# Compression's first product in float32 from unsplit weights, and three moves of work around it

## The chip, the cores and the metric

One NeuronCore of a Trainium2 chip runs the whole program. The metric is device time in microseconds; the median of the timed runs counts, and lower is better.

## What is computed

The program is two transformer layers with attention of several kinds, then two more with other kinds and feed-forward parts, on 256 tokens of width 1024, all in float32. The change lies in the first mixer, native sparse attention (NSA), and in what is loaded around it. Cut to that:

```python
def adaln_norm(x, c, g, w_ada, b_ada):
    mod = jax.nn.silu(c) @ w_ada + b_ada
    shift, scale, gate = jnp.split(mod, 3, axis=-1)
    h = rms_norm(x, g) * (1.0 + scale[:, None, :]) + shift[:, None, :]
    return h, gate[:, None, :]

def nsa_mixer(h, w_in, pe_k, pe_v, ck_w1, ck_w2, cv_w1, cv_w2, w_out):
    u = h @ w_in                       # q, k_c, v_c, k_s, v_s, k_w, v_w, z, gate logits
    ...
    n_cmp = (T - CMP_LEN) // CMP_STRIDE + 1                       # 15 blocks of 32 tokens
    cmp_idx = CMP_STRIDE * np.arange(n_cmp)[:, None] + np.arange(CMP_LEN)[None, :]

    def compress(a, pe, w1, w2):       # w1: 2048 x 256, w2: 256 x 64
        blk = a[:, cmp_idx] + pe[:, None, :]
        blk = jnp.moveaxis(blk, 3, 2).reshape(B, n_cmp, G, CMP_LEN * DH)
        return jax.nn.silu(blk @ w1) @ w2

    k_cmp = compress(k_c, pe_k, ck_w1, ck_w2)
    v_cmp = compress(v_c, pe_v, cv_w1, cv_w2)
    ...
```

`blk @ w1` is a product of 30 rows (15 blocks, two key heads) by 2048 by 256, once for keys (m = 0) and once for values (m = 1).

## The kernel before, in words

**Split weights.** Large products run in fp32r, a faster reading of float32, on pairs: a weight unit of 128 x 1024 floats (512 KB) is loaded into a raw tile (`wraw`, 5 buffers), ScalarE copies it to a high part (`whi`), VectorE subtracts to get a low part (`wlo`), 8 buffers each. Three matmuls (high by high, low by high, high by low) make one product. `specs` lists all units in the order of use; `make` loads and splits the next one, and `pump` runs ahead as long as fewer than 8 units are made and not yet used. All loads go through SyncE's queue (SP), which issues in order and waits at a load whose buffer is not yet free.

**The order of work.** The program is written with priorities (`first(n)`), and a scheduler then fixes the order on each engine before the program runs. Each engine takes its instructions strictly in that order. A move of one line can therefore move others.

**The stages that matter here.** First stage: for each of 8 slices k of the width, the modulation weights `ada_w` (two raw tiles) and the first columns of `w_nsa` (keys, values, gates, half of the queries) are loaded, `modulate(k)` makes a slice of the normed input on ScalarE and VectorE, `multiply(k)` adds its products to six PSUM banks `accp`. Then `dense_cols` makes the other half of the queries ("the q product"), with `kvd` copies and transposes, `blk` (keys and values in blocks, plus positions), and `k_side` and `q_side` (rotation on VectorE, the rotated queries' sum on GpSimd, transposes on TensorE into PSUM banks 6 and 7 in turn, copies out by ScalarE or VectorE). Then come `compress(0)`, `compress(1)` and between them the first "z product" (`zs`). After `compress(1)` the pools are closed, and `ada_rows` loads 24 pieces of 512 KB (`ar`), each multiplied on VectorE (L660) beside the attention.

In `compress` of the kernel before, each of 16 slices j gives three matmuls with the blocks (128 x 30) as the loaded weights and 256 columns of `w1` streaming; the result, 30 x 256, goes through silu and two transposes to `hT`.

In the rows, `wh`/`wl` are the high and low parts of a unit, `wr` its raw tile, `kvd` the doubled keys and values, `q` the queries (their first half, `qf`, plain, their second, `qq`, rotated), `kd` rotated keys, `rt` parts of a rotation, `th`/`h` silu, `m`/`mask` the attention masks, `ar`/`ac` modulation rows.

## Time and profile before

| | |
|---|---|
| time, median of 3 runs | 1000.05 us (994.53 to 1003.32) |
| the profiled execution | 994.04 us, span of its trace 992.3 us |
| TensorE busy (PE) | 934.9 us, 94% of the span |
| VectorE (DVE), ScalarE (ACT) | 701.5 us (71%), 538.8 us (54%) |
| DMA | 177.66 MB, mean 179 GB/s |

Busy time is the time in which an engine has an instruction in work; matmuls overlap, so a busy TensorE isn't at its peak. The granted clock is TensorE's: 1.00 is full speed (2.4 GHz), 0.50 half of it.

### The profile page before, as it was taken

What the parts mean: (1) busy time and instruction counts of PE and PEld (TensorE: products, weight loads), DVE (VectorE), ACT (ScalarE), POOL (GpSimd) and SP (SyncE); (2) the same over time, 40 slices, a digit from 0 to 9 for tenths busy, and PEclk for the clock granted to TensorE, in tenths of its full rate; (3) what the DMA queues carried; (4) which work ended last, traced back from release to release, by engine and by line L of the source; (5) the groups of instructions that cost most, each with busy time, mean ns of one, the idle gap of its engine ahead of it and who ended that gap; (6) DMA issues with size and microseconds to landing.
All of it is one profiled execution on the core that took longest, in us unless ns stands there. A gap on an engine that the chain in (4) does not pass through costs nothing.

```text
span 992.3 us, 14766 instructions
## 1 busy us (share of the span) xinstructions
PE 934.9 (94%) x5316; PEld 783.7 (79%) x5316; DVE 701.5 (71%) x1454; ACT 538.8 (54%) x1062; POOL 40.6 (4%) x49
## 2 busy tenths in 40 slices
PE   5997998899999998999799999999999899999996
PEld 4876786687778877967788888887997688888885
DVE  5888899858777768586857565677466676665655
ACT  5584567834545626486346554435676355555540
POOL 1003000001120001000000000000000000000000
PEclk9998798999999999999999999999999999999999
DMA  9996787334855425632356554655635243565541
GB/s 288 304 311 217 221 269 253 108 106 151 261 202 182 149 66 197 236 111 86 95 203 212 170 184 159 241 181 151 221 132 152 90 167 126 193 235 170 182 137 43
DMA packets 106169, 177.66 MB, mean 179 GB/s; under 512 B 8816, under 2 KB 40688, under 8 KB 106096
## 3 DMA queue, kind: packets, MB, share of 16 engines
q1 hardware_dynamic: 106096, 176.72, 54.6%
q8 instruction: 42, 0.69, 0.3%
q14 instruction: 31, 0.25, 0.1%
HBM read 175.65 MB, written 1.05 MB: 178 GB/s over the span
## 4 chain that ended last, share of the span: by engine, by line
PE 77%; DVE 11%; ACT 5%; DMA 4%; issue 2%; SPq 1%; POOL 0%; DVEq 0%; ACTq 0%; POOLq 0%
PE ps L279 15%; PE ps L239 13%; PE ps L240 13%; PE ps L243 13%; PE ps L280 8%; DVE wl L211 2%; DMA wr<-in_ada_w_dram 2%; PE ps L469 2%; PE ps L320 1%; DVE ac L660 1%; PE ps L839 1%; PE ps L525 1%; ACT e L482 1%; PE ps L297 1%; PE ps L298 1%
## 5 line engine op out<-in xcount | busy, mean ns | idle before, releaser
L211 DVE TENSOR_TENSOR wl<-wr,wh 128x1024 fp32r<-128x1024 f32 (+5 forms) x276 | 319.6, 1195 | 78.7 <-ACT wh L210 77.3
L210 ACT ACTIVATE wh<-wr 128x1024 fp32r<-128x1024 f32 (+5 forms) x276 | 270.6, 1021 | 72.4 <-PE ps L243 21.2
L279 PE MATMUL ps<-xhl,wh 128*128 128x512 f32 x640 | 226.5, 398 | 0.0
L239 PE MATMUL ps<-wh,xhl 128*128 128x512 f32 (+5 forms) x544 | 197.4, 375 | 4.5 <-ACT xhl L312 2.4
L240 PE MATMUL ps<-wl,xhl 128*128 128x512 f32 (+5 forms) x544 | 199.0, 368 | 0.0
L280 PE MATMUL ps<-xhl,wl 128*128 128x256 f32 x640 | 179.2, 281 | 0.0
L243 PE MATMUL ps<-wh,xhl 128*128 128x512 f32 (+5 forms) x544 | 172.9, 370 | 0.9 <-DVE xhl L313 0.6
L279 PEld LDWEIGHTS ps<-xhl,wh 128*128 128x128 f32 x640 | 120.0, 188 | 28.9
L280 PEld LDWEIGHTS ps<-xhl,wl 128*128 128x128 f32 x640 | 120.9, 189 | 1.1
L239 PEld LDWEIGHTS ps<-wh,xhl 128*128 128x128 f32 x544 | 103.6, 192 | 22.8 <-ACT xhl L312 5.1
L240 PEld LDWEIGHTS ps<-wl,xhl 128*128 128x128 f32 x544 | 104.5, 192 | 14.0 <-issue 0.2
L243 PEld LDWEIGHTS ps<-wh,xhl 128*128 128x128 f32 x544 | 99.8, 190 | 18.2 <-DVE xhl L313 2.4
L1124 ACT ACTIVATE hs<-ps 128x256 f32<-128x256 f32 x80 | 30.0, 377 | 100.1 <-PE ps L280 100.1
L1125 DVE TENSOR_TENSOR hs<-ps,hs 128x256 f32<-128x256 f32 x80 | 32.6, 420 | 68.4 <-ACT hs L1124 68.4
L243 PE MATMUL ps<-wh,hl 128*128 128x512 f32 x176 | 68.3, 390 | 0.0
L240 PE MATMUL ps<-wl,hh 128*128 128x512 f32 x176 | 68.3, 390 | 0.0
L239 PE MATMUL ps<-wh,hh 128*128 128x512 f32 x176 | 66.7, 390 | 0.0
L482 ACT ACTIVATE e<-e,sm 128x128 f32<-128x128 f32 x112 | 49.6, 445 | 12.7 <-DVE sm L476 12.6
L312 ACT ACTIVATE xhl<-ps 128x512 fp32r<-128x512 f32 x28 | 16.5, 597 | 67.9 <-PE ps L309 67.8
L476 DVE CUSTOM_DVE_ANT_0 e<-ps,mask 128x128 f32<-128x128 f32 (+1 forms) x144 | 44.1, 350 | 8.8 <-PE ps L489 4.3
L660 DVE SCALAR_TENSOR_TENSOR ac<-ar,cs,ac 128x512 f32<-128x512 f32 x56 | 42.7, 764 | 4.0 <-DMA ar<-in_ada_w_dram 3.7
L334 POOL TENSOR_TENSOR sm<-sm,nhalf 128x1 f32<-128x1 f32 x18 | 13.2, 734 | 721.3 <-DVE sm L333 721.3
(315 smaller groups left out, 1299.3 us busy)
## 6 DMA issues: line engine op xcount, KB each, us to landing
wr<-in_ffn_w_gate_dram SPq DMA_DIRECT2D x44, 512.0 KB, 4.7
wr<-in_ffn_w_up_dram SPq DMA_DIRECT2D x44, 512.0 KB, 4.7
wr<-in_ffn_w_down_dram SPq DMA_DIRECT2D x44, 512.0 KB, 5.0
ar<-in_ada_w_dram SPq DMA_DIRECT2D x32, 512.0 KB, 4.5
wr<-in_dil_w_in_dram SPq DMA_DIRECT2D x32, 512.0 KB, 4.6
wr<-in_cd_w_in_dram SPq DMA_DIRECT2D x22, 512.0 KB, 4.4
wr<-in_ada_w_dram SPq DMA_DIRECT2D x32, 256.0 KB, 4.9
...
```

The source lines that it names most:

```text
L210: act.activation(hi, raw[:, :nk * n], AF.Copy)
L211: dve.tensor_sub(lo, raw[:, :nk * n], hi.bitcast(F32))
L239: pe.matmul(p, lhsT=xt[0][:, k, :], rhs=w[0][:, kw, c], start=start and t == 0, stop=False)
L240: pe.matmul(p, lhsT=xt[0][:, k, :], rhs=w[1][:, kw, c], start=False, stop=False)
L243: pe.matmul(p, lhsT=xt[1][:, k, :], rhs=w[0][:, kw, c], start=False, stop=stop and t == n - 1)
L279: pe.matmul(p, lhsT=w[0], rhs=xhl[:, k].rearrange("p a t -> p (a t)"), start=k == 0, stop=False)
L280: pe.matmul(p[:, :256], lhsT=w[1], rhs=xh[:, k, :], start=False, stop=k == 7)
L476: state["dve"] = dve.tensor_tensor_reduce(out=e[:, c0:c1], in0=s[:, c0:c1], in1=added[:, 256 - (c1 - c0):], scale=-scale, scalar=3e38, op0 ...
L482: act.activation(e[:, c0:c1], e[:, c0:c1], AF.Exp, bias=n2[:, i:i + 1], scale=-1.0, accum_out=den[:, i:i + 1])
L660: dve.scalar_tensor_tensor(ac, raw[:, j, :], cs[:, k:k + 1], ac, op0=ALU.mult, op1=ALU.add)
L1124: act.activation(t[:, c], p[:, 256:], AF.Copy)
L1125: dve.tensor_add(t[:, c], p[:, :256], t[:, c])
```

## The change

Five edits. (1) The units of `ck_w1` and `cv_w1` become "whole" units: 2048 x 256 in two units a matrix, loaded as float32 straight into the buffers of `whi` and `wlo` (half of a unit in each), with no raw tile and no split; `compress` takes 2 units in place of 4. (2) The product is turned round: 128 x 128 pieces of `w1` are the loaded weights, the 30 blocks stream, in float32, 2 halves by 16 slices; silu's result is `hT` itself, so the two transposes, their copy and the split of `blk` go; factors of 0.5 move into later copies. (3) `ident`, `ccol`, `gcol` and `bcol` are issued from ScalarE's queue. (4) `w2k`, `w2v` and the masks are issued behind the last load that has been made by then; `peT` stays ahead, behind `cc`. (5) The keys and values are rotated and copied out ahead of the queries.

```diff
     ident = cp.tile([128, 128], F32, name="ident")
-    nc.sync.dma_start(ident, A["k_ident"])
+    nc.scalar.dma_start(ident, A["k_ident"])
...
-    nc.sync.dma_start(ccol, A["c_col"])
+    nc.scalar.dma_start(ccol, A["c_col"])
...
     def make():
-        W, k0, nk, cols = specs[len(made)]
+        W, k0, nk, cols, whole = specs[len(made)]
         n = sum(b - a for a, b in cols)
+        if whole:
+            parts = []
+            for i, tag in enumerate(("whi", "wlo")):
+                t = wp.tile([128, UNIT], F32R, tag=tag, bufs=NB, name=nm("ww")).bitcast(F32).rearrange("p (k n) -> p k n", n=n)
+                h = t.shape[1]
+                a, b = cols[0]
+                state["dma"] = nc.sync.dma_start(t, W[(k0 + i * h) * 128:(k0 + (i + 1) * h) * 128, a:b].rearrange("(k p) n -> p k n", p=128))
+                parts.append(t)
+            made.append(parts)
+            return
...
-    spec_cols(A["nsa_ck_w1"][0], 16, [[(0, 256)]])
-    spec_cols(A["nsa_cv_w1"][0], 16, [[(0, 256)]])
+    for name in ("nsa_ck_w1", "nsa_cv_w1"):
+        for k0 in (0, 8):
+            spec(A[name][0], k0, 8, [(0, 256)], True)
...
         nc.sync.dma_start(cc, A["k_cc"])
+        nc.sync.dma_start(peT, A["pe_T"])
     pump()
-    load_masks()
-    nc.sync.dma_start(peT, A["pe_T"])
-    for j in range(2):
-        nc.sync.dma_start(w2k[:, :, j * 64:(j + 1) * 64], A["nsa_ck_w2"][0].rearrange("(k p) n -> p k n", p=128))
-    nc.sync.dma_start(w2v, A["nsa_cv_w2"][0].rearrange("(k p) n -> p k n", p=128))
+    with behind(state["dma"]):
+        for j in range(2):
+            nc.sync.dma_start(w2k[:, :, j * 64:(j + 1) * 64], A["nsa_ck_w2"][0].rearrange("(k p) n -> p k n", p=128))
+        nc.sync.dma_start(w2v, A["nsa_cv_w2"][0].rearrange("(k p) n -> p k n", p=128))
+        load_masks()
...
-    blk = [(pB.tile([128, 16, 30], F32R, name=f"blkh{m}"), pB.tile([128, 16, 30], F32R, name=f"blkl{m}")) for m in range(2)]
+    blk = [pB.tile([128, 16, 30], F32, name=f"blk{m}") for m in range(2)]
...
-            act.activation(hi, f, AF.Copy)
-            dve.tensor_sub(lo, f, hi.bitcast(F32))
...
     with first(SINK):
         for tok in range(2):
-            q_side(tok, 1, accp[4 + tok])
-        for tok in range(2):
-            k_side(accp[tok], tok, 256, 384, 0)
             p = accp[2 + tok]
             act.activation(vS[:, tok, :], p[:, 0:128], AF.Copy)
             k_side(p, tok, 128, 256, 1)
             act.activation(vW[:, tok, :], p[:, 256:384], AF.Copy)
             act.activation(gates[:, tok, :], p[:, 384:432], AF.Tanh, scale=0.5)
+        for tok in range(2):
+            q_side(tok, 1, accp[4 + tok])
+        for tok in range(2):
+            k_side(accp[tok], tok, 256, 384, 0)
...
     def compress(m, tp):
-        ws = get(4)
+
+        ws = get(2)
         p = ps("c")
-        for j in range(16):
-            w, l = ws[j // 4], blk[m]
-            for i, (a, b) in enumerate(((0, 0), (0, 1), (1, 0))):
-                pe.matmul(p[:30, :256], lhsT=l[a][:, j, :], rhs=w[b][:, j % 4, :],
-                          start=j == 0 and i == 0, stop=j == 15 and i == 2)
-        done(4)
-        h2 = tp.tile([128, 256], F32, tag="h2", bufs=1, name=nm("h2"))
-        silu2(p[:30, :256], h2[:30], tp)
+        for half in range(2):
+            for j in range(16):
+                w = ws[j // 8][j % 8 // 4][:, j % 4, half * 128:(half + 1) * 128]
+                pe.matmul(p[:, half * 30:(half + 1) * 30], lhsT=w, rhs=blk[m][:, j, :], start=j == 0, stop=j == 15)
+        done(2)
         hT = tp.tile([128, 2, 30], F32, tag="hT", bufs=2, name=nm("hT"))
-        p = ps("pt")
-        for j in range(2):
-            pe.transpose(p[:, j * 30:(j + 1) * 30], h2[:30, j * 128:(j + 1) * 128], ident[:30, :30])
-        act.activation(hT, p[:, :60].rearrange("p (j n) -> p j n", j=2), AF.Copy, scale=0.5)
+        silu2(p[:, :60], hT.rearrange("p j n -> p (j n)"), tp)
         return hT
```

**What the scheduler makes of it** at three places. Line numbers above 160 differ between the two kernels: L205 is now L216 and L209 (the whole units), L210 is L221, L320 is L331, L323 is L334, L812 is L821, L839 is L850, L868 is L873.

*Place 1, SP's queue* after the loads of the q product. Before:

```order
L205 DMA wr133_663<-in_nsa_ck_w1_dram 128x4x256
L205 DMA wr136_669<-in_nsa_ck_w1_dram 128x4x256
L205 DMA wr173_843<-in_nsa_ck_w1_dram 128x4x256
L205 DMA wr176_849<-in_nsa_ck_w1_dram 128x4x256
L205 DMA wr186_907<-in_nsa_cv_w1_dram 128x4x256
L205 DMA wr189_919<-in_nsa_cv_w1_dram 128x4x256
L205 DMA wr192_931<-in_nsa_cv_w1_dram 128x4x256
L205 DMA wr195_943<-in_nsa_cv_w1_dram 128x4x256
L205 DMA wr204_1018<-in_nsa_w_in_dram 128x2x512
L153 DMA ab288_1344<-in_ada_b_dram 128x1024
L205 DMA wr207_1024<-in_nsa_w_in_dram 128x2x512
```

and now:

```order
L209 DMA ww135_668<-in_nsa_ck_w1_dram 128x4x256
L209 DMA ww169_831<-in_nsa_cv_w1_dram 128x4x256
L209 DMA ww171_835<-in_nsa_cv_w1_dram 128x4x256
L209 DMA ww134_666<-in_nsa_ck_w1_dram 128x4x256
L209 DMA ww136_670<-in_nsa_ck_w1_dram 128x4x256
L780 DMA w2k_103<-in_nsa_ck_w2_dram 128x2x64 x2
L781 DMA w2v_104<-in_nsa_cv_w2_dram 128x2x64
L162 DMA m137_675<-in_k_mask_dram 128x544
L162 DMA m138_678<-in_k_mask_dram 128x544
L209 DMA ww170_833<-in_nsa_cv_w1_dram 128x4x256
L209 DMA ww172_837<-in_nsa_cv_w1_dram 128x4x256
L216 DMA wr189_927<-in_nsa_w_in_dram 128x2x512
```

Three of the four z units of the first z product now stand ahead of this piece (behind the q units), the masks and `w2` stand in it, and the fourth z unit, `wr189`, is last.

*Place 2, ScalarE* when `multiply(7)` ends. Before:

```order
L210 ACTIVATE wh122_641<-wr121_639 128x1024
L210 ACTIVATE wh125_647<-wr124_645 128x1024
L782 ACTIVATE kvd141_720<-ps11_162 128x512
L823 ACTIVATE vS_99<-ps13_164 128x128
L812 ACTIVATE q147_752<-ps15_166 128x512
L782 ACTIVATE kvd143_729<-ps12_163 128x512
L210 ACTIVATE wh128_653<-wr127_651 128x1024
L823 ACTIVATE vS_99<-ps14_165 128x128
L812 ACTIVATE q152_772<-ps16_167 128x512
L210 ACTIVATE wh131_659<-wr130_657 128x1024
```

and now:

```order
L221 ACTIVATE wh122_642<-wr121_640 128x1024
L221 ACTIVATE wh125_648<-wr124_646 128x1024
L221 ACTIVATE wh128_654<-wr127_652 128x1024
L795 ACTIVATE kvd139_714<-ps11_162 128x512
L829 ACTIVATE vS_99<-ps13_164 128x128
L795 ACTIVATE kvd141_723<-ps12_163 128x512
L221 ACTIVATE wh131_660<-wr130_658 128x1024
L829 ACTIVATE vS_99<-ps14_165 128x128
L802 ACTIVATE kvT_712<-ps140_716 64x4x127
L802 ACTIVATE kvT_712<-ps142_725 64x4x128
```

The third split (`wh128`) now stands ahead of both `kvd` copies. On TensorE the transposes of both copies now stand ahead of the whole q product; before, one stood ahead of it and one among its products.

*Place 3, ScalarE and TensorE* during the q product's end and `compress(0)`. ScalarE before, from the value weights' splits on:

```order
L210 ACTIVATE wh190_921<-wr189_919 128x1024
L210 ACTIVATE wh193_933<-wr192_931 128x1024
L812 ACTIVATE q198_949<-ps185_900 128x512
L323 ACTIVATE qp11_113<-ps155_780 128x512
L210 ACTIVATE wh196_945<-wr195_943 128x1024
L825 ACTIVATE vW_100<-ps13_164 128x128
L826 ACTIVATE gates_101<-ps13_164 128x48
L210 ACTIVATE wh205_1020<-wr204_1018 128x1024
L825 ACTIVATE vW_100<-ps14_165 128x128
L826 ACTIVATE gates_101<-ps14_165 128x48
L323 ACTIVATE kT_98<-ps160_799 128x2x128
```

and now:

```order
L334 ACTIVATE qp01_111<-ps154_776 128x512
L221 ACTIVATE wh187_917<-wr186_915 128x1024
L821 ACTIVATE q192_933<-ps179_884 128x512
L221 ACTIVATE wh190_929<-wr189_927 128x1024
L334 ACTIVATE qp11_113<-ps159_796 128x512
L334 ACTIVATE kT_98<-ps164_815 128x2x128
L221 ACTIVATE wh199_988<-wr198_986 128x1024
L334 ACTIVATE kT_98<-ps168_826 128x2x128
L221 ACTIVATE wh202_994<-wr201_992 128x1024
L334 ACTIVATE qp00_110<-ps177_872 128x512
L579 ACTIVATE th205_999<-ps197_953 128x60
```

TensorE before:

```order
L320 MATMUL ps155_780<-ident_67,q152_772 128x128 x4
L320 MATMUL ps151_766<-ident_67,q147_752 128x128 x4
L839 MATMUL ps203_969<-wh134_665,blkh0_711 30x256
L839 MATMUL ps203_969<-wl135_666,blkh0_711 30x256
L839 MATMUL ps203_969<-wh134_665,blkl0_712 30x256
L839 MATMUL ps203_969<-wh134_665,blkh0_711 30x256
L839 MATMUL ps203_969<-wl135_666,blkh0_711 30x256
L839 MATMUL ps203_969<-wh134_665,blkl0_712 30x256
```

and now:

```order
L850 MATMUL ps197_953<-blk0_707,ww133_664 128x30 x4
L850 MATMUL ps197_953<-blk0_707,ww134_666 128x30 x2
L331 MATMUL ps159_796<-ident_67,q156_788 128x128 x4
L850 MATMUL ps197_953<-blk0_707,ww134_666 128x30
L331 MATMUL ps160_802<-ident_67,q156_788 128x128 x4
L850 MATMUL ps197_953<-blk0_707,ww134_666 128x30
L850 MATMUL ps197_953<-blk0_707,ww135_668 128x30 x4
L850 MATMUL ps197_953<-blk0_707,ww136_670 128x30 x4
L850 MATMUL ps197_953<-blk0_707,ww133_664 128x30 x2
L331 MATMUL ps164_815<-ident_67,kd161_808 128x128 x2
L850 MATMUL ps197_953<-blk0_707,ww133_664 128x30 x2
L850 MATMUL ps197_953<-blk0_707,ww134_666 128x30 x4
```

On ScalarE the split `wh190` of the fourth z unit now stands ahead of the copy `qp11`, which empties the PSUM bank that TensorE's `ps164` takes next. On TensorE the transposes of the first rotated queries (before `ps151`, from `q147`) stood right ahead of the first compression product; now they stand earlier, among the q product, and those of the second token block (`q156`) and of `kd161` stand inside the compression.

## Rows read from the trace of the kernel before

**Rows 1.** Windows: busy us of PE, PEld, DVE, ACT, POOL; clock, DMA share, GB/s.
```profile
3.00:25.00 22.00, 13.34 (x50) 11.90 (x51) 13.31 (x36) 13.08 (x25) 3.36 (x6) 1.00 1.07 317
25.00:53.00 28.00, 25.15 (x139) 21.90 (x138) 24.16 (x61) 16.81 (x35) 0.00 (x0) 1.00 1.04 313
53.00:82.00 29.00, 22.86 (x113) 19.13 (x113) 25.39 (x41) 21.75 (x33) 1.70 (x2) 0.94 0.95 313
```

**Rows 2.** Chain that ended last, 30 to 125 us: start, length, what.
```profile
76.84 0.67 DVE rt L440
...
80.83 4.05 PE ps L839 x19
...
86.79 0.44 PE ps L320 x4
...
97.34 1.27 PE ps L839 x11
```

**Rows 3.** Timeline of TensorE, 50 to 112 us: start, length, instruction, [idle before].
```profile
60.29 0.65 PE L785 MATMUL ps<-ident,kvd 128*128 128x128 f32 x4
...
79.71 1.11 PE L320 MATMUL ps<-ident,q 128*128 128x128 f32 x4 [6.14 <-POOL q L447]
```

**Rows 4.** The same timeline at the end of the compression.
```profile
104.75 0.41 PE L880 MATMUL ps<-kbd,qp 128*128 128x30 f32 x2 [1.25 <-ACT kbd L860]
...
106.92 1.86 PE L868 MATMUL ps<-w2v,rep 128*120 128x64 f32 x8 [0.65 <-ACT rep L867]
109.21 1.65 PE L469 MATMUL ps<-kT,qr 64*128 64x128 f32 x8 [0.43 <-DVE cs L886]
```

**Rows 5.** Waits of SP's queue, 0 to 130 us: waiting line, releaser, us, times.
```profile
SPq L638 <- PE ps L868: 3.0, 1, 3.0
```

**Rows 6.** Windows of the attention stage, columns as in rows 1.
```profile
114.00:150.00 36.00, 36.00 (x219) 27.46 (x219) 34.47 (x113) 25.50 (x74) 0.00 (x0) 0.97 0.78 254
150.00:193.00 43.00, 38.04 (x261) 28.98 (x262) 40.06 (x153) 35.53 (x120) 0.00 (x0) 0.92 0.62 199
```

**Rows 7.** DMA issues of 0 to 210 us: count, KB each, us to landing.
```profile
m<-in_k_mask_dram SPq DMA_DIRECT2D x2, 272.0 KB, 5.2
...
w2k<-in_nsa_ck_w_dram SPq DMA_DIRECT2D x2, 64.0 KB, 4.3
...
w2v<-in_nsa_cv_w_dram SPq DMA_DIRECT2D x1, 64.0 KB, 4.6
```

**Rows 8.** Timeline of SP, its first issue and the masks.
```profile
0.73 0.39 SPq L128 DMA_DIRECT2D ident<-in_k_ident_dram  x1
...
11.08 0.91 SPq L162 DMA_DIRECT2D m<-in_k_mask_dram  x2
```

**Rows 9.** Groups by form, 50 to 125 us: count, busy us, mean ns.
```profile
L211 DVE TENSOR_TENSOR wl<-wr,wh 128x1024 fp32r<-128x1024 f32 x24 | 29.3, 1235 | 9.0 <-ACT wh L210 9.0
L210 ACT ACTIVATE wh<-wr 128x1024 fp32r<-128x1024 f32 x24 | 25.4, 1059 | 9.6 <-issue 4.0 <-PE ps L839 2.3 <-DMA wr<-in_nsa_w_in_dram 2.0
...
L796 DVE TENSOR_TENSOR blk<-kvT,peT 128x240 f32<-128x240 f32 x4 | 2.0, 563 | 0.0
```

**Rows 10.** Timeline of TensorE at full clock, 132 to 139 us.
```profile
135.81 0.39 PE L880 MATMUL ps<-kbd,qp 128*128 128x30 f32 x2
136.04 0.18 PE L881 MATMUL ps<-cmask,identb 128*128 128x30 bf16 x1
```

**Rows 11.** Timeline of ScalarE, 55 to 115 us.
```profile
56.36 1.06 ACT L210 ACTIVATE wh<-wr 128x1024 fp32r<-128x1024 f32 x1 [0.75 <-DMA wr<-in_nsa_w_in_dram]
58.68 1.06 ACT L210 ACTIVATE wh<-wr 128x1024 fp32r<-128x1024 f32 x1 [1.26 <-DMA wr<-in_nsa_w_in_dram]
```

**Rows 12.** Windows of one microsecond, and one stretch of attention, columns as in rows 1.
```profile
80.00:81.00 1.00, 1.00 (x6) 0.91 (x6) 1.00 (x2) 0.00 (x0) 0.00 (x0) 0.50 1.03 383
...
112.00:113.00 1.00, 1.00 (x7) 1.00 (x8) 0.08 (x1) 0.00 (x0) 0.00 (x0) 0.50 1.03 393
...
186.00:199.00 13.00, 11.07 (x87) 8.58 (x86) 9.75 (x39) 11.44 (x39) 0.00 (x0) 1.00 0.18 70
```

More of the change, by code (lines that the diff above doesn't have):

```diff
@@ L184, in behind, with spec @@
         return nullcontext() if ins is None else tc.issue_after(ins.ins)
-    def spec(W, k0, nk, cols):
-        specs.append((W, k0, nk, cols))
+    def spec(W, k0, nk, cols, whole=False):
+        specs.append((W, k0, nk, cols, whole))
     def spec_cols(W, nk, groups):
```

12 lines of the change are left out of this document (5 added, 7 removed).

## The prediction

> **What bounds the kernel now.** I read the windows of the first 82 us first. From 3 us on the DMA engines are full (share 0.95 to 1.07, 313 to 317 GB/s), while VectorE and TensorE are not [rows 1]: the first stage runs at the pace of its loads. Next, the chain of waits: at 76.84 it lies on VectorE (rotation of queries, behind eight splits of compression weights), and from 80.83 on TensorE [rows 2]. Between them TensorE's timeline shows the price: 6.14 us idle until 79.71, for the rotated queries' sum on GpSimd [rows 3], and after it half clock (its window of 80 to 81) [rows 12]. At the end of the compression it idles again, 1.25 and 0.65 us [rows 4]. Then SP's waits: the first `ar` load waits for L868, the last product that reads the compression's pools [rows 5], and from 114 to 193 us VectorE is busy 74.5 of 79 us [rows 6], much of it with the `ar` pieces. So the end of L868, 108.8 us [rows 4], is where a shift of this stage reaches the rest: what is won there moves all that follows. In the order of the changed kernel everything behind the first mixer stands as before, but for a handful of rows. I sum up to that point.
>
> **First stage, loads.** The masks and `w2` are issued at 11 us and later among the first stage's loads [rows 8]; they leave it: 2 x 272 + 2 x 64 + 64 = 736 KB [rows 7], at 313 GB/s 2.4 us. Bounds: 0 (if VectorE bound this stage) and 2.4; I take 2.4, as the share of 1.04 says. They come back behind the compression's key weights, beside the work of that stage. SP's issue of `ident` (0.39 us) no longer stands ahead of `x` [rows 8]: 0.4. The other three small issues, 1.2 us more at that length, I count at nothing: from 3 us on the engines are full [rows 1], so an earlier issue only lengthens the line. The Trainium skill has a rule for this (DMA: Bandwidth & Descriptors, "Issuing engines are not separate DMA queues"): loads of every issuing engine run on the same 16 engines and interleave, and a second issuer saves issue time alone. The trace agrees in that the share doesn't rise above full; if the second queue brought bandwidth, the whole 1.6 us would count. **Sum: -2.8.**
>
> **Removed waits.** Eight splits go, 1.24 us each on VectorE and 1.06 on ScalarE [rows 9], 9.9 and 8.5 us, with the two splits of `blk`. They stand ahead of the rotation that TensorE waits for; with them go the 6.1 us [rows 3]. What is late next there is below. After the idle time 19 products take 4.05 us at half clock, where eleven take 1.27 at full clock [rows 2]: 0.213 against 0.115, 1.8 us; the four transposes take 1.11 [rows 3], later 0.44 [rows 2]: 0.6 with rounding. **-8.5.** The gaps of 1.25 and 0.65 us and half clock on L868 (1.86 us for eight, half of it 0.9) go if TensorE gets there fed [rows 4]: **-2.8.**
>
> **The product turned round.** Before: 96 matmuls of 0.115 us at full clock [rows 2], 11.0. After: 64 float32 products with 128 x 128 loaded weights and 30 columns. The trace has this very form: L880, two rows each, 135.81 to 136.04 [rows 10], 0.23 us. 64 x 0.23 = 14.7. The four short transposes go, four tenths of a microsecond at the pace of rows 2. All of it is on TensorE's path: **+3.2** with rounding. A price below 0.23 has no row; the same form at half clock would be 0.46 (first rival).
>
> **New waits.** The order shows four. (a) Place 2: both `kvd` transposes wait for ScalarE, where the third q split stands first. Its weights: the two units before it landed at 56.36 and 58.68 [rows 11]; 512 KB at 313 GB/s take 1.7, so 60.4, less 2.8 is 57.6. Split 1.06 [rows 11] and a copy of half its width, about 0.6, give 59.3, the second copy and transposes 60.3. `multiply(7)` ends at 60.29 - 2.8 = 57.5 [rows 3], and eight transposes are 0.9: **+1.9** (0 if ScalarE's split were early; 3 at most). (b) The transposes of `kd` stand inside the q product's first token block. VectorE must first have `blk` (four of 0.56, 2.0 us in all [rows 9]) and rotate keys, for the second `kd` also a query block (0.67 for the first of three steps [rows 2]); TensorE comes there after 19 products of 0.23, at 64.7, the two `kd` by my count at 65.7 and 67.4: **+1.8** (0 to 3). (c) Place 3: `ps164` waits for `qp11`, which waits behind `wh190` for the fourth z unit. By the shapes in the code, what stands in SP's queue up to that unit is 24.6 MB; by rows 1 the engines move 24.8 MB between 3 and 82 us (79 us at 313 to 317 GB/s), some before 3, and start 0.4 earlier, so it lands near 80.5. Split 1.06 and copy 0.6: 82.2. TensorE comes there at 60.3 + 48 products (11.0) + 1.8 + 20 transposes (2.2, rows 2) + 18 products (4.1) = 79.4: **+2.8** (0 to 6). (d) After `compress(1)` VectorE splits one more unit (1.24) before `hT`, with ScalarE's tanh and copies after it; six z products (1.4) cover part: **+1.0.**
>
> Edits at nothing: (3)'s loads on ScalarE, which waits for `x` anyway; silu on 128 x 60 instead of 30 x 256; the moved factors; GpSimd's mask copies, now between the second and third sum of queries, with the masks there by about 77 us and the third sum not needed before 83. The whole units' loads wait for buffers that `multiply(6)` and `multiply(7)` leave at 57.5; behind them in SP's queue stands the fourth z unit of (c), nothing else that is early enough to matter.
>
> **After L868** TensorE is at half clock still: L469's eight take 1.65 us [rows 4], at full clock half of it, 0.8, and the four L880 pairs behind them, 0.25 with L881 at full clock [rows 10] and twice that here, another 1.0. If TensorE comes there fed, 1.8 go; it comes there behind gaps of 1 to 3 us, so I take half, **-0.9**.
>
> **Sum:** -2.8 - 8.5 - 2.8 + 3.2 + 1.9 + 1.8 + 2.8 + 1.0 - 0.9 = **-4.3**; with (a) to (c) at their lower bounds -10.8, at their upper ones +1.2. I keep the middle. The profiled execution, 994.04 (span 992.3 and 1.7 around it), would be near 990; it lies 6 us under the median, so against the median of 1000.05 the forecast is **996**.
>
> **Rivals.** *The float32 product runs at half clock.* 64 loads of full weights with 30 columns each are little work for the array. For it: from 109 to 116 us TensorE is busy with such small float32 products, and the clock stays at 0.50 (window of 112 to 113) [rows 12]. Against it: 13 us of attention with float32 products of 64 columns and transposes alone, busy 85%, have 1.00 [rows 12]. The price is 64 x 0.23 = 14.7 more: 996 + 14.7 = 1010.7. It turns the gain into a loss from 19 products at half clock on (4.3 / 0.23). The Trainium skill (TensorE: Matmul & The Clock Gate, "Part 1: The HAM clock gate") has the clock follow how busy TensorE has been; whether loading weights counts it doesn't say, and only the stretch with 1.00 bears on that.
>
> *The new waits cost little.* If z's fourth unit lands by 78 and VectorE has both `kd` early, (b) and (c) go, 4.6 us, and TensorE, without a gap of some us, keeps full clock behind L868, the other 0.9. -4.3 - 4.6 - 0.9 = -9.8 gives 990.2. For it: the fourth z unit is the only late one; against it: DMA full until 82 [rows 1].
>
> *The waits take the place of the one removed.* A gap of (c)'s size drops the clock as the one of 6.14 did; its tail cost 2.4 (above), and the fourth z unit, behind masks and value weights, may land 2.5 later. Then 996 + 4.9 = 1001: no change.
>
> **How the numbers follow.** Chances: forecast 0.40, waits cheap 0.28, waits instead 0.22, half clock 0.10. The runs before spread from 994.5 to 1003.3, so 1% (10 us) is about what this measurement can tell. Faster by more than that needs less than 990.05: half of the second rival and a little of the forecast's spread, 0.20. Slower needs 1010: half of the first, 0.06. The rest, 0.74, is within. The range reaches from the cheap waits with a fast run, 986, to the third rival with the runs' spread, 1003; half clock and the far end of the cheap waits stay out.
>
> **What would show it.** In the trace after: the DMA share full from 3 us and `multiply(7)` over near 57.5; no gap of 6 us before the compression; pairs of rows of the new product at 0.23 us and granted clock 1.00; gaps before the `kvd` and `kd` transposes and before `ps164`, with ScalarE waiting for the z unit's DMA; L873 over near 105, and the first `ar` load right after it; the same distance at the end of the first mixer and of the program. Wrong would make it: a clock of 0.50 in the compression; an attention stage that doesn't keep the shift, since VectorE or a load bounds it otherwise; a first stage that isn't shorter.

## The result, and the profile after

The changed kernel takes 1005.73 us (median of 12 runs, 1001.81 to 1013.06), the kernel before 998.5 (12 runs on the same chip, 994.18 to 1003.32): a ratio of 1.0081, 95% interval 1.0053 to 1.0109. It is 7.2 us slower, where 4 us less was forecast. The profiled execution took 1006.06 us (span 1004.2, mean clock 0.965). That of before, 994.04, lies 4.5 us under its own median, so of the 11.9 us between the two spans more than 4 are the choice of the run.

TensorE's clock is the first thing to look at. This is the page's line of the granted clock in 40 slices of 25 us, in the profile after:

```profile
PEclk9988597999999999999899999999999979999999
```

The fifth slice (100 to 126 us, the second compression and the start of attention) is at 5 tenths, the fourth (75 to 100 us) at 8. The windows show what the engine did there. Columns as in rows 1, instructions in brackets.

```profile
3.00:25.00 22.00, 13.58 (x48) 11.78 (x49) 14.60 (x39) 14.94 (x28) 1.11 (x2) 1.00 1.07 304
...
53.00:82.00 29.00, 25.49 (x128) 21.25 (x127) 25.07 (x49) 16.57 (x29) 8.92 (x8) 0.88 1.04 349
86.00:88.00 2.00, 2.00 (x15) 2.00 (x14) 0.72 (x1) 1.70 (x3) 0.00 (x0) 0.67 0.52 173
88.00:92.00 4.00, 4.00 (x13) 3.31 (x14) 1.39 (x3) 0.22 (x1) 0.00 (x0) 0.50 0.59 208
...
94.00:100.00 6.00, 6.00 (x54) 5.70 (x52) 0.76 (x2) 1.31 (x5) 0.00 (x0) 1.00 0.00 0
100.00:102.00 2.00, 2.00 (x14) 2.00 (x13) 0.21 (x1) 0.00 (x0) 0.00 (x0) 0.58 0.00 0
102.00:120.00 18.00, 17.57 (x73) 15.56 (x74) 8.23 (x27) 5.61 (x17) 0.00 (x0) 0.50 0.43 147
...
114.00:150.00 36.00, 35.86 (x210) 27.57 (x207) 31.82 (x109) 22.97 (x67) 0.00 (x0) 0.91 0.77 249
150.00:193.00 43.00, 38.80 (x241) 28.61 (x240) 39.76 (x141) 31.89 (x106) 0.00 (x0) 0.84 0.66 209
```

The DMA engines are as full as in rows 1. From 86 to 88 and from 100 to 102 us the clock falls to half (0.50, 1.2 GHz) while TensorE is busy all of the time (2.00 of 2.00 us) and no gap precedes. In attention the clock is lower than before, 0.91 and 0.84 against 0.97 and 0.92 [rows 6], with VectorE no busier. A part of that is the choice of the run as well: the profiled execution of before has 34 us at half clock, where its runs have 46 to 52 as a median (table below).

TensorE's timeline from the end of the first stage to the end of the compression (start, length, instructions, idle before and what ended it):

```profile
57.53 1.38 PE L254 MATMUL ps<-wh,xhl 128*128 128x384 f32 x6
60.24 1.31 PE L798 MATMUL ps<-ident,kvd 128*128 128x128 f32 x8 [1.33 <-ACT kvd L795]
63.73 0.79 PE L250 MATMUL ps<-wh,xhl 128*128 128x512 f32 x1 [2.18 <-ACT q L821]
64.33 0.63 PE L251 MATMUL ps<-wl,xhl 128*128 128x512 f32 x1
...
69.76 0.39 PE L250 MATMUL ps<-wh,xhl 128*128 128x512 f32 x1
...
81.21 2.54 PE L850 MATMUL ps<-blk,ww 128*128 128x30 f32 x22
...
87.03 1.33 PE L850 MATMUL ps<-blk,ww 128*128 128x30 f32 x6
...
99.74 9.05 PE L850 MATMUL ps<-blk,ww 128*128 128x30 f32 x44
...
111.30 1.71 PE L873 MATMUL ps<-w2v,rep 128*120 128x64 f32 x8
113.44 1.65 PE L480 MATMUL ps<-kT,qr 64*128 64x128 f32 x8 [0.43 <-DVE cs L891]
```

Here stand the main differences. The gaps of 6.14 us [rows 3] and of 1.25 and 0.65 us [rows 4] are gone. In their place are 1.33 us for `kvd` (the prediction's wait (a)) and 2.18 us for the copy of the queries, L821, which no step had. Behind it a 512-column product takes 0.63 us as shown, later, at 69.76, 0.39. The turned product takes 0.108 us a row at full clock (22 rows from 81.21 to 83.59, where the next instruction starts), 0.22 a product, as priced; the 44 rows from 99.74 to 108.60 take 0.20 each, since most of them run at half clock. L873 is over at 113.0 us instead of 108.8 [rows 4], and in SP's queue the first `ar` load follows at once:

```profile
113.08 1.39 SPq L650 DMA_DIRECT2D ar<-in_ada_w_dram  x3
```

So 4.2 us of the 7.2 are there when the compression ends; the other 3 come later.

ScalarE's timeline shows why the copies of the queries, which must empty the banks of PSUM that the q product takes next, come so late: they stand last, behind a split of weights and the copies of `kvT`.

```profile
60.73 1.07 ACT L221 ACTIVATE wh<-wr 128x1024 fp32r<-128x1024 f32 x1
61.67 0.29 ACT L829 ACTIVATE vS<-ps 128x128 f32<-128x128 f32 x1
61.98 1.08 ACT L802 ACTIVATE kvT<-ps 64x508 f32<-64x508 f32 x2
63.08 1.08 ACT L821 ACTIVATE q<-ps 128x512 f32<-128x512 f32 x2
```

### The profile page after: what moved, and what is told of

Its sections match the earlier page's. It is cut to its first block, busy times and chain, and to the rows that moved or that the text cites. A ratio compares the mean times of both kernels' runs of the same rounds, so it can differ in the third digit from the quotient of the medians.

```text
span 1004.2 us, 14783 instructions
## 1 busy us (share of the span) xinstructions
PE 952.6 (95%) x5344; PEld 801.1 (80%) x5344; DVE 694.4 (69%) x1444; ACT 528.7 (53%) x1050; POOL 42.5 (4%) x49
## 4 chain that ended last, share of the span: by engine, by line
PE 78%; DVE 10%; DMA 6%; ACT 4%; issue 2%; SPq 0%; POOL 0%; DVEq 0%; ACTq 0%; POOLq 0%
PE ps L290 15%; PE ps L250 13%; PE ps L254 13%; PE ps L251 13%; PE ps L291 8%; DMA wr<-in_ada_w_dram 2%; PE ps L850 2%; PE ps L480 2%; PE ps L331 2%; DVE wl L222 1%; PE ps L320 1%; PE ps L536 1%; ACT e L493 1%; DVE ac L672 1%; PE ps L309 1%
## 5 line engine op out<-in xcount | busy, mean ns | idle before, releaser
L222 DVE TENSOR_TENSOR wl<-wr,wh 128x1024 fp32r<-128x1024 f32 (+5 forms) x268 | 311.0, 1197 | 80.6 <-ACT wh L221 68.9
L221 ACT ACTIVATE wh<-wr 128x1024 fp32r<-128x1024 f32 (+5 forms) x268 | 262.1, 1020 | 77.6 <-PE ps L254 24.7
L250 PE MATMUL ps<-wh,xhl 128*128 128x512 f32 (+5 forms) x544 | 206.9, 384 | 8.2 <-ACT xhl L323 2.7
L251 PE MATMUL ps<-wl,xhl 128*128 128x512 f32 (+5 forms) x544 | 202.9, 376 | 0.0
L254 PE MATMUL ps<-wh,xhl 128*128 128x512 f32 (+5 forms) x544 | 173.9, 377 | 0.9 <-DVE xhl L324 0.6
L250 PEld LDWEIGHTS ps<-wh,xhl 128*128 128x128 f32 x544 | 107.6, 198 | 27.8 <-ACT xhl L323 5.3
L251 PEld LDWEIGHTS ps<-wl,xhl 128*128 128x128 f32 x544 | 107.8, 198 | 13.9
L254 PEld LDWEIGHTS ps<-wh,xhl 128*128 128x128 f32 x544 | 103.3, 197 | 18.1 <-DVE xhl L324 2.4
L493 ACT ACTIVATE e<-e,sm 128x128 f32<-128x128 f32 x112 | 49.6, 444 | 12.7 <-DVE sm L487 12.7
L323 ACT ACTIVATE xhl<-ps 128x512 fp32r<-128x512 f32 x28 | 16.4, 597 | 70.1 <-PE ps L320 70.0
```

Source lines behind the costliest of these rows:

```text
L221: act.activation(hi, raw[:, :nk * n], AF.Copy)
L222: dve.tensor_sub(lo, raw[:, :nk * n], hi.bitcast(F32))
L250: pe.matmul(p, lhsT=xt[0][:, k, :], rhs=w[0][:, kw, c], start=start and t == 0, stop=False)
L251: pe.matmul(p, lhsT=xt[0][:, k, :], rhs=w[1][:, kw, c], start=False, stop=False)
L254: pe.matmul(p, lhsT=xt[1][:, k, :], rhs=w[0][:, kw, c], start=False, stop=stop and t == n - 1)
L493: act.activation(e[:, c0:c1], e[:, c0:c1], AF.Exp, bias=n2[:, i:i + 1], scale=-1.0, accum_out=den[:, i:i + 1])
```

## The experiments

Theory A: the turned product, with its 30 moving columns for each 128 x 128 of loaded weights, takes TensorE's clock to half with the engine busy, in both compressions, and the low clock makes them late. Theory B: the order of the keys causes the wait for `q`, and that wait with its half clock is the loss. Rival C: the moved loads cost what the product gains. All runs in one table; the ratio is to the kernel before, run on the same chip. "First `ar`" is read from the one profiled execution of each kernel, so that differences of one or two microseconds can be that execution's own. "Half clock" is twice what the mean granted clock lacks of 1, times the span, as a median over the runs.

| kernel | median us | ratio [95%] | first `ar`, us | half clock, us |
|---|---|---|---|---|
| before | 997.4 to 998.7 | | 108.8 | 46 to 52 |
| after | 1005.73 | 1.0081 [1.0053, 1.0109] | 113.1 | 69 |
| e1 120 columns | 991.54 | 0.9946 [0.9917, 0.9974] | 106.0 | 35 |
| e2 queries first | 1007.15 | 1.0068 [1.0035, 1.0100] | 112.1 | 68 |
| e3 256 columns, turned back | 993.33 | 0.9956 [0.9935, 0.9978] | 106.7 | 38 |
| e4 before + moved loads | 991.26 | 0.9933 [0.9906, 0.9961] | 104.2 | 39 |
| e5 e1 + early `q` copies | 994.54 | 0.9963 [0.9936, 0.9990] | 108.1 | 36 |
| e6 e4 + keys' order | 993.0 | 0.9946 [0.9918, 0.9973] | 105.5 | 42 |
| e7 after without moved loads | 1000.2 | 1.0021 [0.9992, 1.0051] | 109.6 | 58 |
| e8 e4 + turned, split weights | 1021.26 | 1.0233 [1.0195, 1.0271] | 129.3 | 88 |
| e9 120 columns in `compress(1)` only | 1000.07 | 1.0030 [1.0003, 1.0056] | 108.6 | 50 |
| e10 e1, masks later | 989.87 | 0.9922 [0.9895, 0.9950] | 102.2 | 31 |
| e11 e4, masks later | 999.97 | 1.0035 [1.0008, 1.0062] | 109.9 | 44 |
| e12 after, masks later | 998.88 | 1.0006 [0.9985, 1.0027] | 109.1 | 51 |
| e13 e1, `compress(1)`'s product twice | 998.51 | 1.0013 [0.9987, 1.0039] | 111.2 | 34 |
| e14 e3, masks later | 990.84 | 0.9933 [0.9907, 0.9958] | 102.5 | 38 |

**e1: the same product with 120 columns.** `blk` gets four blocks of zeros at its end, and each product moves four blocks of columns instead of one. Of each result the first 30 columns are used; the other 90 are read by nothing. The silu step behind it is written anew for the wider layout.

```diff
-                pe.matmul(p[:, half * 30:(half + 1) * 30], lhsT=w, rhs=blk[m][:, j, :], start=j == 0, stop=j == 15)
+                pe.matmul(p[:, half * 120:(half + 1) * 120], lhsT=w, rhs=blk[m].rearrange("p j n -> p (j n)")[:, j * 30:j * 30 + 120], start=j == 0, stop=j == 15)
```

> The changed kernel, but each float32 product of the compression moves 120 columns instead of 30: its own 30 and the 90 that lie behind them in the blocks' tile (results of the 90 are not read; the products are as many, the loaded weights the same). Theory A (the clock under the turned product costs the time): the granted clock stays at 1.00 through both compressions instead of falling to 0.50 near 87 and near 101 us; half clock cost about 2.6 us from 87 to 93 and 6 to 8 us from 101 to 120, so the last product on rep (L873, 113.0 in the changed kernel) ends near 105 and the whole is 6 to 9 us shorter than the changed kernel: ratio to the kernel before 0.999 to 1.002. Theory B (TensorE's wait for ScalarE's copies ahead of the q product, and its half clock, cost the time): nothing of that is touched, the ratio stays at 1.008 and the clock falls as before.

It is 14 us faster than the changed kernel, where theory A had 6 to 9, and faster than the one before. About half of the 14.2 stands at the first `ar` (7.1 us), the rest comes later. Its windows at the places of the two falls:

```profile
86.00:88.00 2.00, 2.00 (x20) 2.00 (x19) 1.23 (x1) 1.44 (x3) 0.00 (x0) 1.00 0.87 324
...
92.00:100.00 8.00, 8.00 (x71) 7.70 (x70) 0.97 (x2) 1.31 (x5) 0.00 (x0) 1.00 0.08 31
100.00:102.00 2.00, 2.00 (x20) 2.00 (x20) 0.66 (x1) 1.06 (x1) 0.00 (x0) 1.00 0.00 0
```

and two rows of its TensorE timeline:

```profile
64.56 0.79 PE L250 MATMUL ps<-wh,xhl 128*128 128x512 f32 x1 [2.18 <-ACT q L823]
...
81.82 2.39 PE L852 MATMUL ps<-blk,ww 128*128 128x120 f32 x20
```

The clock stays at 1.00 through both compressions. Four times the columns cost nothing: 20 rows from 81.82 to 84.05 are 0.112 each, against 0.108 for 30 columns. The wait of 2.18 us is still there: it is not what separates the two kernels. Nor is the new silu step: e3 below keeps full clock without it. Theory A holds; B can explain only a part.

**e2: queries first**, the old order of rotation in the changed kernel.

```diff
+        for tok in range(2):
+            q_side(tok, 1, accp[4 + tok])
         for tok in range(2):
+            k_side(accp[tok], tok, 256, 384, 0)
             p = accp[2 + tok]
...
-        for tok in range(2):
-            q_side(tok, 1, accp[4 + tok])
-        for tok in range(2):
-            k_side(accp[tok], tok, 256, 384, 0)
```

> The changed kernel with the old order of rotations (queries first, then keys, then values). Theory B: the first q product no longer waits 2.18 us for ScalarE's copy of the queries, the clock does not fall to 0.50 from 63 to 69 us, the q product ends 4 to 6 us earlier (74 instead of 78.9), and the whole is 4 to 6 us shorter: ratio to the kernel before 1.002 to 1.004. Theory A: the same up to there, but the clock still falls to 0.50 under both compressions; if A holds the larger share, the gain behind the second compression is under 3 us: ratio 1.005 to 1.008.

No difference from the changed kernel that these intervals show. The wait remains in TensorE's timeline,

```profile
63.44 0.76 PE L331 MATMUL ps<-ident,q 128*128 128x128 f32 x4 [2.27 <-ACT q L821]
```

and the second compression falls to half clock again, without an idle moment:

```profile
98.00:110.00 12.00, 12.00 (x57) 11.71 (x57) 2.86 (x4) 2.33 (x3) 0.00 (x0) 0.50 0.13 45
```

One half of theory B falls: the order of the keys doesn't make the wait. What the wait costs, this run can't say; e12 does.

**e3: unsplit weights, product turned back**, so that 256 columns move for each loaded block of `blk`.

```diff
-        for half in range(2):
-            for j in range(16):
-                w = ws[j // 8][j % 8 // 4][:, j % 4, half * 128:(half + 1) * 128]
-                pe.matmul(p[:, half * 30:(half + 1) * 30], lhsT=w, rhs=blk[m][:, j, :], start=j == 0, stop=j == 15)
+        for j in range(16):
+            pe.matmul(p[:30, :256], lhsT=blk[m][:, j, :], rhs=ws[j // 8][j % 8 // 4][:, j % 4, :], start=j == 0, stop=j == 15)
```

> The changed kernel with the product turned back: blocks of 30 columns as loaded weights, the unsplit float32 weights moving in 256 columns, 16 products for each compression, then tanh, two transposes and a copy as in the kernel before. A float32 product of 256 columns has no row; four times the 0.115 of the old one is 0.46, 7.4 us for each compression as 32 of 0.23 are now, and the transposes and copies behind add about 1 us twice. Theory A: the clock stays at 1.00 there, the end of the last product on rep moves from 113.0 to about 107, ratio 1.000 to 1.004. Theory B: no gain, ratio 1.008 to 1.010.

Its windows of the two products:

```profile
77.00:86.00 9.00, 9.00 (x44) 4.36 (x42) 6.84 (x8) 4.80 (x6) 4.52 (x6) 1.00 1.00 368
...
92.00:100.00 8.00, 8.00 (x42) 4.16 (x41) 2.61 (x3) 2.92 (x4) 0.00 (x0) 1.00 0.19 63
```

Float32 weights without the turn keep full clock. So neither the float32 operands nor the missing splits are the cause.

**e4: the moved loads alone**, on the kernel before.

```diff
-    nc.sync.dma_start(ident, A["k_ident"])
+    nc.scalar.dma_start(ident, A["k_ident"])
...
+    with behind(state["dma"]):
...
+        load_masks()
```

> The kernel before with the moved loads alone (ident and the three small columns on ScalarE's queue; w2 and the masks behind the compression's first weight units). The prediction's term: the first stage ends 2.8 us earlier, and so does what follows it, ratio 0.997. What the changed kernel's trace shows: the last first-stage product ends 1.5 us earlier, ratio 0.9985. A rival: the masks and w2 come back beside the compression's weights while the DMA is still full, the splits that TensorE waits for move with them, and nothing is won: 1.000.

This part by itself gains 6.9 us. Its TensorE timeline has the rotated queries' sum (L447) with 0.42 us of idle time in place of 6.14 [rows 3]:

```profile
81.81 0.66 PE L320 MATMUL ps<-ident,q 128*128 128x128 f32 x4 [0.42 <-POOL q L447]
```

and VectorE's timeline tells why: the rotation starts at 71.32 us, behind three of the eight splits, where it started at 76.84 [rows 2], behind seven (the eighth follows at 79.04).

```profile
71.32 0.68 DVE L440 TENSOR_TENSOR rt<-q,cc 128x512 f32<-128x512 f32 x1
```

The splits themselves are all still there. What ended the gap is their order on VectorE. Rival C falls in this plain form.

**e5: the queries' copies ahead** of the `kvT` copies on ScalarE, in e1.

```diff
+        for tok in range(2):
+            early.append(wide("q"))
+            copied = act.activation(early[tok][:, :512], accp[4 + tok], AF.Copy)
...
+            with behind(copied):
                 act.activation(kvT[64:128, ...
```

> The kernel with 120 columns and, in addition, ScalarE's two copies of the queries out of PSUM ahead of its copies into kvT. Theory B for what is left (TensorE waits 2.18 us at 64.56 for those copies and then runs at 0.50 until 70): the wait shrinks by the length of the kvT copies, to about 1.1 us, as in the kernel with the moved loads alone, where 1.31 us left the clock at 1.00; with 6 us of half clock gone too that is 1.1 + 3 = 4 us less, ratio to the kernel before 0.990 to 0.992. Rival: the transposes of the queries now stand behind kvT's work and the splits of the z units land no earlier (DMA full until 88 us), so TensorE waits there instead: ratio 0.994 as without this edit.

The wait of 2.18 us shrinks to 0.94 and the q product runs at full clock, yet the kernel is no faster than e1 (the intervals overlap). TensorE's and ScalarE's timelines show where it went:

```profile
82.34 1.11 PE L331 MATMUL ps<-ident,q 128*128 128x128 f32 x4 [4.12 <-ACT qp L334]
```

```profile
80.75 1.06 ACT L221 ACTIVATE wh<-wr 128x1024 fp32r<-128x1024 f32 x1 [3.56 <-DMA wr<-in_nsa_w_in_dram]
```

This is wait (c) of the prediction: `qp` behind the split of z's fourth unit, which landed near 80.7 (forecast 80.5). In the changed kernel TensorE came there too late to meet it. Behind the gap the clock is at 0.50 (82 to 84 us), with 120 columns too.

**e6: moved loads and the keys' order, old product.** The rotation blocks of the diff on e4.

```diff
         for tok in range(2):
-            q_side(tok, 1, accp[4 + tok])
...
+        for tok in range(2):
+            q_side(tok, 1, accp[4 + tok])
```

> The moved loads and the key-first order with the old product (split weights, 96 products of 256 columns for both compressions). It parts the change: the kernel with the moved loads alone has 0.9933. If the key order is worth nothing, 0.993; if ScalarE's later copies of the queries (theory B) are the key order's fault, 2 to 5 us more, 0.995 to 0.998. Against the changed kernel (1.008) it gives the price of the unsplit, turned product with its clock; against the one with 120 columns (0.9946) the price of that product at full clock: theory A has the first at 12 to 15 us and the second at 0 to 2 us.

Within the intervals it is e4: the order of the keys costs nothing that can be measured. From here the turned product with unsplit weights makes the changed kernel: 1005.7 - 993.0 = +12.7 us; with 120 columns (e1) -1.5, with 256 (e3) +0.3.

**e7: the changed kernel without the moved loads.**

```diff
-    nc.scalar.dma_start(ident, A["k_ident"])
+    nc.sync.dma_start(ident, A["k_ident"])
...
-        load_masks()
```

> The changed kernel with the loads where they stood before (ident and small columns first on SP's queue, masks and w2 in the first stage). If the loads' 6.9 us add to the rest, 1.008 + 0.007 = 1.015. If what the loads alone won was the wait before the compression (rotation behind eight splits), which the unsplit weights remove as well, only the shorter first stage is lost, 1.5 us: 1.009 to 1.010.

The loads that gain 6.9 us alone cost 5.5 here. Its windows:

```profile
58.00:74.00 16.00, 15.69 (x78) 12.86 (x76) 12.23 (x23) 11.34 (x21) 0.10 (x1) 1.00 1.07 370
...
84.00:98.00 14.00, 14.00 (x113) 13.10 (x113) 6.12 (x10) 4.79 (x11) 1.64 (x2) 1.00 0.37 126
...
100.00:116.00 16.00, 13.73 (x62) 12.28 (x62) 7.98 (x26) 5.17 (x14) 0.00 (x0) 0.50 0.48 164
```

No wait before the q product: it belongs to the moved loads, by the order that they give ScalarE. The first compression runs at half clock from 76 to 82 us, behind waits of 0.20 and 0.38 us. From 84 to 98 us, with transposes and other products between runs of 2 to 18 rows of the turned product, the clock stays at 1.00; in the run of 44 rows, from 97.75 on, it falls. So the form doesn't bring the clock down wherever it stands.

**e8: the turned product with the old split weights**, three terms, 192 products, on e4: theory A's wide form, without float32.

```diff
+        for half in range(2):
+            for j in range(16):
+                w = ws[j // 4]
+                for i, (a, b) in enumerate(((0, 0), (0, 1), (1, 0))):
+                    pe.matmul(p[:, half * 30:(half + 1) * 30], lhsT=w[b][:, j % 4, half * 128:(half + 1) * 128], rhs=l[a][:, j, :],
+                              start=j == 0 and i == 0, stop=j == 15 and i == 2)
```

> The kernel with the moved loads alone, and in it the product turned round with the split weights kept: 192 products with loaded weights of 128 x 128 and 30 columns, three for each block of weights, instead of 96 with loaded blocks and 256 columns. One such product was not seen; a weight load took 0.104 us in the other kernels, so some 0.11 each, 10.6 us for each compression against 5.6, 10 us more in all at full clock. Theory A in its narrow form (what the clock falls under is the float32 operands of the turned product): the clock stays at 1.00 in both compressions, ratio 0.993 + 0.010 = 1.003. In its wide form (it falls under the turned product, whatever the operands): 0.50 in both compressions as in the changed kernel, 6 to 10 us more, ratio 1.009 to 1.013.

```profile
78.00:80.00 2.00, 2.00 (x15) 2.00 (x15) 2.00 (x3) 0.38 (x1) 2.00 (x1) 0.66 0.96 368
80.00:98.00 18.00, 18.00 (x84) 17.60 (x85) 11.54 (x22) 5.89 (x10) 3.89 (x3) 0.50 0.59 176
...
106.00:122.00 16.00, 16.00 (x81) 16.00 (x80) 3.42 (x4) 2.11 (x2) 0.00 (x0) 0.50 0.10 31
```

In these windows the clock falls from 78 to 80 us with TensorE busy all of the time, and is at half again from 106 on, each time under the turned product. So the fall doesn't need float32; the turned form was enough. The kernel is 30.0 us slower than e4, where 16 to 20 were forecast: 10.3 are the products at full clock (192 of 0.111 for 96 of 0.115), as priced; at half clock it runs not for a part of the stage but for 20 us from 78.7 on and for 23 from 106.0 to the first `ar`.

**e9: 120 columns in the second compression only.**

```diff
+        n = 120 if m else 30
```

> The changed kernel with 120 columns in the second compression only (values); the first keeps 30. It parts the 14.2 us between the two falls of the clock. By the trace of the changed kernel half clock lasted from 86.7 to 93.4 behind the first compression (3.4 us lost at most) and from 100.8 to 120.5 in and behind the second (up to 9.8): the second fall carries most, ratio 0.997 to 1.000; if the first carries most, 1.002 or more.

```profile
84.00:92.00 8.00, 8.00 (x36) 7.61 (x36) 3.15 (x4) 3.31 (x5) 0.00 (x0) 0.50 0.61 225
94.00:106.00 12.00, 12.00 (x101) 11.49 (x100) 2.47 (x5) 3.64 (x8) 0.00 (x0) 1.00 0.04 14
```

In these windows the second compression keeps full clock, and the kernel is 5 us better than the changed one. The first falls to half as before, but here behind 1.66 us of idle time for `qp`, so that this run can't say what of the other 8.5 us (to e1) is that wait, nor, as its forecast meant it to, which of the two falls costs more.

**e10, e11, e12, e14: the masks' load later**, among z's weights instead of among the compression's, in e1, e4, the changed kernel and e3.

```diff
-        load_masks()
     multiply(7)
...
     dense_cols(xt, 8, 512, lambda tok, p: q_side(tok, 0, p))
+    with behind(state["dma"]):
+        load_masks()
```

> The kernel with 120 columns and the masks still later in SP's queue, among z's weights instead of ahead of the value weights. The queries' copies stand earlier in ScalarE's order here (the first between the two copies of keys and values). Theory B for the rest: no wait of 2.18 us and no half clock from 64 to 70 us; together with z's weights 1.7 us earlier, the first ar load moves from 106.0 to 102 to 104, ratio 0.990 to 0.993. Rival (the stage up to 88 us is bound by the DMA engines, which were full there, and TensorE only waits at another place): the first ar load stays at 105 to 107, ratio 0.994 to 0.996.

> The kernel before with moved loads and the old product, the masks as late as in the run with 120 columns beside it. By theory B a little less than with the loads alone (TensorE waited 1.31 us there for the queries' copies, at full clock): 0.991 to 0.993. By the rival no difference: 0.993 to 0.995.

> The changed kernel (30 columns) with the masks as late as in the run with 120 columns and late masks: the fourth corner of a square of two edits (30 or 120 columns; masks where the change put them, or later), whose other corners have 1.0081, 0.9946 and 0.9922. Theory A alone: the clock still falls to 0.50 in both compressions; later masks are worth here what they are with 120 columns, 2 to 3 us, ratio 1.005 to 1.007. Theory B (the wait for ScalarE's copies, gone here as in the changed kernel without the moved loads, which has 1.0021): 6 us less, ratio 1.001 to 1.003.

> The product turned back with unsplit weights (256 columns) and the masks late, against the same masks with 120 columns (0.9922): the products take as long, and transposes and copies lie between them and what follows. If the later masks are worth as much here as there (2 to 4 us against 0.9956), 0.992 to 0.994; if ScalarE's and VectorE's steps behind the products (tanh, transposes, copies) then stand on the path, 0.995 to 0.997.

e10 has the lowest median of all, and its windows of the two compressions show full clock:

```profile
72.00:90.00 18.00, 17.27 (x127) 15.86 (x127) 15.43 (x30) 7.45 (x16) 11.95 (x8) 1.00 1.01 348
90.00:98.00 8.00, 8.00 (x78) 8.00 (x78) 2.02 (x4) 2.50 (x4) 0.20 (x2) 1.00 0.14 51
```

e11 turns the gain of e4 into a loss: VectorE's rotation stands behind seven of the eight splits again, and TensorE's gap is back. It ends now with ScalarE's copy of `gates`, which stands behind a wait for VectorE's rotation of the keys (3.04 us, until 77.86).

```profile
75.56 0.68 DVE L440 TENSOR_TENSOR rt<-q,cc 128x512 f32<-128x512 f32 x1
```

```profile
78.30 0.42 PE L841 MATMUL ps<-wh,blkh 128*30 128x256 f32 x1 [5.37 <-ACT gates L826]
```

So the place of a 0.5 MB load decides, through the order written from it, what VectorE does first. In e12 the wait for `q` goes, and the clock falls all the same in both compressions, the first time three microseconds after 0.62 us of idle time, the second without any:

```profile
60.00:74.00 14.00, 13.57 (x68) 11.09 (x68) 10.42 (x22) 9.81 (x19) 1.65 (x1) 1.00 1.08 348
...
78.00:90.00 12.00, 12.00 (x50) 11.12 (x50) 8.61 (x13) 2.71 (x4) 5.77 (x4) 0.50 0.77 280
...
104.00:116.00 12.00, 9.73 (x43) 8.07 (x43) 7.85 (x27) 4.62 (x16) 0.00 (x0) 0.51 0.67 218
```

Its ratio, 1.0006, is what theory B forecast (1.001 to 1.003), not what A alone did (1.005 to 1.007): in the changed kernel the wait and the half clock behind it are a part of the loss as well. e14, at 0.9933, lies where the later masks were forecast to be worth as much as with 120 columns.

At the first `ar` the two edits add up: from 113.1 us the later masks take 4.0 (e12), 120 columns 7.1 (e1), both 10.8 (e10). In the medians they don't: -6.9, -14.2, -15.9.

**e13: the second compression's product computed twice**, in e1: 32 products more, 7.4 us at full clock, the same result.

```diff
-        for half in range(2):
+        for half in (0, 1, 0, 1) if m else (0, 1):
```

> The kernel with 120 columns, its second compression computed twice in a row (the first result is overwritten): 32 products of 0.23 us more, 7.4 us at full clock, ahead of the first ar load, which so comes at about 113.4, as late as in the changed kernel (113.08), but with the clock at 1.00 on the way. If every microsecond by which this stage ends later costs one at the end, whatever the clock: 991.5 + 7.4 = 998.9, ratio 1.002. If the stage behind it costs as much again when it starts later (as the medians of the other runs against their first ar load suggest, some 1.5 us for each): 1002 to 1006, ratio 1.004 to 1.008, and half clock is only how the changed kernel gets late. If it stays at 995 or less, TensorE's time in this stage is not what the end waits for.

It asks what lateness alone costs. The two first `ar`, 106.0 and 111.2 us, are 5.2 apart, but the profiled executions differ before the edit already: that of e1 ran below full clock for a while in its first stage, where that of e13 has 1.00, and its first compression product starts 2.2 us later. Rows of e1:

```profile
25.00:40.00 15.00, 13.48 (x68) 12.18 (x68) 12.15 (x33) 7.73 (x17) 0.00 (x0) 0.89 1.01 288
```

```profile
79.40 1.49 PE L852 MATMUL ps<-blk,ww 128*128 128x120 f32 x12
```

and of e13:

```profile
77.15 1.49 PE L852 MATMUL ps<-blk,ww 128*128 128x120 f32 x12
...
95.82 12.30 PE L852 MATMUL ps<-blk,ww 128*128 128x120 f32 x108
```

From that start to the first `ar` are 26.6 us in e1 and 34.1 in e13. So the added products cost 7.5 us there, as priced, and the end comes 7.0 later (998.51 - 991.54), at the same time at half clock (34 and 35 us): lateness costs about one for one, the first of the three forecasts, as far as 7.0 with an interval of some 4 us either way can tell. The changed kernel's first `ar` is 1.9 us later than that of e13, its median 7.2 higher. By that pace some 5 us of the 7.2 go with the clock, 34 us at half clock here and 69 there; this is an estimate from two kernels, which no run of its own shows.

The runs of one and the same kernel point the same way. Among the 12 of the changed kernel the time at half clock reaches from 60 to 89 us, and a straight line through them rises by 0.32 us of time for each us at half clock; among the 35 of the kernel before that ran beside e1 it is 0.34, from 36 to 68 us.

## Why the prediction was wrong

**The step that failed** is "64 x 0.23 = 14.7", "the product turned round". The duration was right (0.22), the clock at which it was taken was not. The first rival, half clock under this product, had 0.10 and came true in part: the clock fell at 86.7 and at 100.3 us (placed by the shares 0.67 and 0.58 of their windows). Half of the time from there to its rise at 93.5 and to the end of L873 at 113.0 is lost, 3.4 + 6.4 = 9.8 us, the z products between among it. The rival had the loss begin at 19 products; some 22 ran at half clock (6 rows of the first compression, 38 or so of the second, two to a product). It priced 14.7 for all 64 products and nothing for their neighbours. e1, e3 and e8 show that it is the turned form with 30 columns: 120 or 256 columns in the same place keep 1.00. In the second compression the clock falls in all five traces that have the 30 columns there (the changed kernel, e2, e7, e8, e12), and in none of the seven with 120 or 256 (e1, e3, e5, e9, e10, e13, e14).

**Why it had only 0.10:** against it I set a stretch of attention at 1.00 [rows 12] whose products have 64 columns, among transposes. The row for it was of the very form, L880, at 0.50 [rows 12]. I read that row as a leftover of an earlier gap, which it may be. L880 fills two short stretches of the trace of before, four pairs each with L881 between: from 104.75 us [rows 4] at 0.25 to 0.27 us a pair, full clock, and from 110.79 at 0.48, half clock.

```profile
105.02 0.39 PE L880 MATMUL ps<-kbd,qp 128*128 128x30 f32 x2
...
111.29 0.61 PE L880 MATMUL ps<-kbd,qp 128*128 128x30 f32 x2
...
111.77 0.61 PE L880 MATMUL ps<-kbd,qp 128*128 128x30 f32 x2
```

Neither is longer than 2 us, so that no row could bear the clock for 64 products in a line, and the 0.10 rested on stretches of another form.

The Trainium skill (TensorE: Matmul & The Clock Gate, "HAM oscillation — how this bites in real kernels") puts such falls down to TensorE idling while it waits for loads. The trace agrees at 63.73 in so far as idle time stands ahead, 1.33 and 2.18 us (there for ScalarE's copies); at 86.7 and 100.3 it doesn't, with 2.00 us of 2.00 busy, and there the measurement decides.

**The waits.** (a) came as forecast (1.33 us; the start of the transposes at 60.24). (b), (c) and (d) did not: -1.8, -2.8 and -1.0. But the wait of 2.18 us for `q` and half clock behind it (14 products of 512 columns at 0.43 a step instead of 0.23, 2.8) is 5.0 that no step had. Place 2 of the order showed that ScalarE's `q` copies had left the piece after `kvd`; I asked only who waits for `kvd`. e2, e7 and e12 show that the masks' new place brings it, not the keys' order.

**The first stage** ends at 58.9 us, 1.4 earlier than the 60.3 of before [rows 3], half of what I took, and inside its bounds.

**"With them go the 6.1 us"** credited the removed splits. e4 removes none of them and loses the gap, for 6.9 us of the median: the gain hung on VectorE's order, which the moved loads alone change. In the changed kernel both causes are present; from e6 to e1 and e3 the removal of the splits itself is worth nothing that can be measured. In e11, where the gap is back, seven of the eight stand ahead of the rotation, as they did before.

**The sum**, up to the end of L873: the forecast without its last term, which lies behind it, is 108.8 - 3.4 = 105.4. Against it stand the first stage +1.4, `q` copies +5.0, (a) to (d) -0.6 - 1.8 - 2.8 - 1.0, the product's price at full clock -0.9 (64 x 0.216 for 14.7) and half clock +9.8, together +9.1; measured 113.0 - 105.4 = +7.6, so within 1.5 us.

**After the compression** I had the shift kept unchanged. 4.2 us became 7.2. By the pace of e13 lateness alone makes about 4.2 of them; the other 3 I put down to more time at half clock, 69 us against 46 to 52; no run shows that by itself. By the third of a microsecond that each costs among runs of one kernel, the 17 to 23 us more would be 5 to 8 us (an estimate), those in the compression, which are in the 4.2 already, among them. In the profiled execution the lower clock stands in attention, 0.91 and 0.84 against 0.97 and 0.92 [rows 6], and not there alone: from 400 to 600 us and from 800 us on it is 0.97, where before it was 0.99. Why the clock falls more often there stays open; also what, beside the form, decides when it falls (e7 ran part of the product at full clock).

**A better version:** e10 at 989.87 beats the kernel before (0.9922) and the changed one by 16 us. Its interval overlaps those of e1, e3 to e6 and e14, so that it is not shown to be better than the moved loads alone.
